# One query tile of two heads at a time in the first block's attention, with the half-array matmuls issued side by side

## The chip, the cores and the metric

The kernel runs on one core of a Trainium2 chip. The metric is the time of one execution in microseconds (us); the median of 3 runs of the kernel before is 2317.44 us (2315.01 to 2317.58). TensorE (PE) multiplies, VectorE (DVE) and ScalarE (ACT) do the elementwise work, GpSimd (POOL) little here, and SyncE (SP) issues most of the DMAs.

## The reference, cut to what matters

Two transformer blocks run one after the other on 256 tokens of width 1024 beside 256 context tokens. The change concerns the first block, which has two layers. Each layer's attention has 8 query heads of 64 numbers and 2 key heads, each shared by 4 query heads. A token sees the context keys and the keys within 128 positions; a learned "sink" joins the sum of each softmax.

```
def sink_softmax(s, sink_b):
    m = jnp.maximum(jnp.max(s, axis=-1, keepdims=True), sink_b)
    e = jnp.exp(s - m)
    return e / (jnp.sum(e, axis=-1, keepdims=True) + jnp.exp(sink_b - m))

s_loc = jnp.where(valid, jnp.einsum('bqkgd,bnkd->bkgqn', qi, ks), -jnp.inf)
s_ctx = jnp.einsum('bqkgd,bnkd->bkgqn', qi, kc)
p = sink_softmax(jnp.concatenate([s_ctx, s_loc], axis=-1), sink_b)
o = einsum('bkgqn,bnkd->bqkgd', p[..., :nc], vc) + einsum('bkgqn,bnkd->bqkgd', p[..., nc:], vs)
```

In the first layer the context tokens are queries as well, over the 256 context keys alone (`context_attention`). In the second layer only the 256 tokens are.

## The kernel before

Activations lie with features on the 128 partitions and tokens along the free dimension. A projection takes each weight as a rounded part and a rest (`wh`, `wl`) and each activation likewise (`xh`, `xl`), and does three matmuls per tile of 128 features (`mm3`, L193 to L195). The parts of a weight chunk are made by ACT (L183) and DVE (L184) from a raw tile that SP's DMA queue has loaded.

The attention is a generator, `attend` (L713), which is advanced by one step each time a projection has finished 128 output columns (`hook`, L731). A step issues `scores` of one call and then `values` of the call before it, so that each softmax has a whole step to finish. A call stands for one pair of heads `t`, one head `hh` of the pair (`t + 4*hh`; head 0 of a pair uses key head 0, head 1 key head 1) and one segment `si`: the 256 tokens (si 0, 512 keys) or the 256 context tokens (si 1, 256 keys, first layer alone). Both 128-row query tiles `i` of the segment are in the call.

`scores` does two matmuls per query tile: one with all 128 rows (L684: the query's rounded part in the head's own 64 rows and its rest in the other 64, against the key's rounded part in both), and one with the head's 64 rows alone (L685: the query's rounded part against the key's rest, `klo`). Results lie in tiles `sc`, of which there are two, each a whole PSUM bank; a call of 256 keys puts both of its query tiles into one. DVE adds the band mask (L688) and takes the maximum (L653); ACT takes the exponential (L657). The rows are then scaled, one tile by ACT (L664) and one by DVE (L666).

`values` transposes the probabilities on PE (L701, 4 or 2 per query tile), has ACT copy one tile and DVE the other from PSUM to `PT` (L702), and then multiplies (L707): weights are 64 columns of `vtok`, so half of the array's columns work, the stream is `PT` with 256 columns, and the sum runs over 4 or 2 blocks of keys. Head 0 writes partitions 0 to 63 of `pso`, head 1 partitions 64 to 127.

A scheduler orders the instructions of each engine by program order and priorities; other matmuls, of the projections and of the modulation vectors (L312, with 32-column weights), are put between the parts of a step. Those L312 matmuls are written so that four consecutive ones use four different strips of 32 array columns.

Of the kernel before, what the change touches and what calls it, by code (L numbers as in the profile page):

```python
# [7 lines left out]
F32 = mybir.dt.float32  # L8
F32R = mybir.dt.float32r
AF = mybir.ActivationFunctionType  # L10
ALU = mybir.AluOpType
AX = mybir.AxisListType
PSUM = bass.MemoryType.PSUM

P = 128
D = 1024
KT = 8
N = 256
T = 512
XS = slice(0, 256)  # L20
CS = slice(256, 512)
# [23 lines left out]
SA = 1  # L45
# [77 lines left out]
class Kern:  # L123
# [67 lines left out]
    def mm3(self, ps, wh, wl, xh, xl, start, stop):  # L191
        mm = self.nc.tensor.matmul
        mm(ps, wh, xh, start=start, stop=False)  # L193
        mm(ps, wh, xl, start=False, stop=False)  # L194
        mm(ps, wl, xh, start=False, stop=stop)  # L195

    def acc(self):
        return self.pacc.tile([P, T], F32, name="acc", tag="acc")
# [380 lines left out]
    def fb_layer(self, l, stats, bga, bgb, AB):  # L579
        nc, I, tc = self.nc, self.I, self.tc  # L580
# [12 lines left out]
        nseg = len(qsegs)  # L593
        fb = self.fb
# [7 lines left out]
        for g in range(4):  # L602
            o = (g % 2) * 64
            nc.scalar.dma_start(wf[o:o + 64, g // 2, o:o + 64], I["w_fourier"][l, g])
        sk = fb.tile([P, 2, 8], F32, name="sk")
        nc.scalar.dma_start(sk[:, 0], I["sink"][l:l + 1, :].to_broadcast([P, 8]))
        nc.vector.tensor_scalar(sk[:, 1], sk[:, 0], -1.0, None, ALU.mult)

        rtmp = lambda: fb.tile([P, 2, T], F32, name="E", tag="E", bufs=EB).rearrange("p a (b n) -> p (a b) n", n=N)
        rows = [slice(0, 64), slice(64, 128)]  # L610
        fr = lambda nm, w_=T: fb.tile([P, w_], F32R, name=nm, tag=nm)
        kh, klo = [fr("kh0"), fr("kh1")], fr("klo")
        vtok = fb.tile([P, 4, P], F32, name="vtok")
        c01 = [self.col(0), self.col(1)]

        def ev_kv(i, ps):
# [7 lines left out]
            else:  # L624
                vT = fb.tile([P, T], F32, name="vT", tag="E", bufs=EB)
                nc.scalar.copy(vT, ps)
# [9 lines left out]
        qs = [[fr(f"qs{t}{j}", TW) for j in range(2)] for t in range(4)]  # L636
# [9 lines left out]
        def q_proj(c, korder=False, hook=None):  # L646
            self.proj(headchunk(0, c), c01, xn, qsegs, lambda i, ps: ev_q(i, ps, c), korder=korder, hook=hook, alloc=None if upd else self.facc)

        def softmax(pss, width, E, h):

            sm = fb.tile([P, 4, 2], F32, name="sft", tag="sft", bufs=3)
            for i, ps in enumerate(pss):
                nc.vector.reduce_max(sm[:, 0, i:i + 1], ps, axis=AX.X)  # L653
            nc.vector.tensor_scalar(sm[:, 1], sm[:, 0], -0.125, sk[:, 1, h:h + 1], ALU.mult, ALU.min)
            nc.vector.tensor_scalar(sm[:, 3], sm[:, 1], sk[:, 0, h:h + 1], None, ALU.add)
            for i, ps in enumerate(pss):
                nc.scalar.activation(E[:, i, 0:width], ps, AF.Exp, bias=sm[:, 1, i:i + 1], scale=0.125,  # L657
                                     accum_out=sm[:, 2, i:i + 1])
            nc.scalar.activation(sm[:, 3], sm[:, 3], AF.Exp)
            nc.vector.tensor_tensor(sm[:, 2], sm[:, 2], sm[:, 3], ALU.add)  # L660
            nc.vector.reciprocal(sm[:, 2], sm[:, 2])
            for i in range(2):
                if i < SA:
                    nc.scalar.activation(E[:, i, 0:width], E[:, i, 0:width], AF.Copy, scale=sm[:, 2, i:i + 1])  # L664
                else:
                    nc.vector.tensor_scalar(E[:, i, 0:width], E[:, i, 0:width], sm[:, 2, i:i + 1], None, ALU.mult)  # L666

        def scores(t, hh, si):
            seg = qsegs[si]
            nk = 4 if si == 0 else 2  # L670
            E = fb.tile([P, 2, T], F32, name="E", tag="E", bufs=EB)
            pss = []
            for i in range(2):
                if si == 0:
                    ps = self.sc()
                elif i == 0:
                    p1 = self.sc()
                    ps = p1[:, 0:256]
                else:
                    ps = p1[:, 256:512]  # L680
                q = qs[t][hh][:, seg.start + i * P:seg.start + (i + 1) * P]
                ks = slice(0, T) if si == 0 else CS
                r = rows[hh]
                nc.tensor.matmul(ps, q, kh[hh][:, ks], start=True, stop=False)  # L684
                nc.tensor.matmul(ps, q[r], klo[r, ks], start=False, stop=True)  # L685
                if si == 0:
                    b = slice((1 - i) * P, (2 - i) * P)
                    nc.vector.tensor_tensor(ps[:, b], ps[:, b], band[:, i * P:(i + 1) * P], ALU.add)  # L688
                pss.append(ps)
            softmax(pss, nk * P, E, t + 4 * hh)  # L690
            return E

        def values(t, hh, si, E, pso):
            seg = qsegs[si]
            nk = 4 if si == 0 else 2
            wd = nk * P
            PT = fb.tile([P, 4, N], F32, name="PT", tag="PT", bufs=2)
            for i in range(2):
                p2 = self.wk()
                for j in range(nk):  # L700
                    nc.tensor.transpose(p2[:, j * P:(j + 1) * P], E[:, i, j * P:(j + 1) * P], self.ident)  # L701
                (nc.scalar.copy if i == 0 else nc.vector.tensor_copy)(  # L702
                    PT[:, 0:nk, i * P:(i + 1) * P], p2[:, 0:wd].rearrange("p (j n) -> p j n", j=nk))
            r = slice(64 * hh, 64 * hh + 64)
            for j in range(nk):
                jj = j if si == 0 else j + 2
                nc.tensor.matmul(pso[r, seg], vtok[:, jj, 64 * hh:64 * hh + 64], PT[:, j, :],  # L707
                                 start=(j == 0), stop=(j == nk - 1))
            if hh == 1 and si == nseg - 1:
                att[t] = f1(f"qs{t}0", TW)  # L710
                nc.scalar.copy(att[t], pso[:, 0:TW])

        def attend():  # L713
            last = None
            for t in range(4):
                pso = None
                for hh in range(2):
                    for si in range(nseg):
                        E = scores(t, hh, si)
                        if last is not None:  # L720
                            values(*last)
                        if pso is None:
                            pso = self.wk()
                        last = (t, hh, si, E, pso)
                        yield
            values(*last)
            yield

        att_gen = attend()

        def hook():  # L731
# [17 lines left out]
        def fourier():  # L749
            for si, seg in enumerate(qsegs):  # L750
                U = fb.tile([P, 2, 2, 2 * P], F32, name="U", tag="PT", bufs=2)
                for tt in range(2):
# [39 lines left out]
        if l == 0:  # L792
# [4 lines left out]
            pss = [[self.facc() for _ in c01] for _ in first]  # L797
# [41 lines left out]
        h = self.xn  # L839
# [32 lines left out]
        ys = [fb.tile([P, 2, T], F32, name="E", tag="E", bufs=EB) for _ in range(3)]  # L872
        ys.append(fb.tile([P, 4, N], F32, name="PT", tag="PT", bufs=2).rearrange("p (a b) n -> p a (b n)", a=2))
        y = [ys[k // 2][:, k % 2, 0:TW] for k in range(KT)]
# [277 lines left out]
    def even_mixer(self, stats):  # L1152
# [10 lines left out]
        with tc.tile_pool(name="ev", bufs=1, reuse_waits="tile") as ev:  # L1163
# [118 lines left out]
            def mlstm():  # L1282
                for hh in range(4):
# [3 lines left out]
                    for dr in range(2):  # L1287
# [3 lines left out]

                        mk = ev.tile([P, 4, P], F32, name="mk", tag="PT", bufs=2)
                        nc.vector.tensor_tensor(mk, pm.rearrange("p (t n) -> p t n", t=4),
# [92 lines left out]
            def dattn(units):  # L1386
                for h, sis in units:
                    c0, hc = h // 2, h % 2
                    for si in sis:
                        nk = 4 if si == 0 else 2  # L1390
                        wd = nk * P
                        for i in range(2):
# [17 lines left out]
                            for j in range(nk):  # L1410
                                nc.tensor.transpose(p2[:, j * P:(j + 1) * P], E[:, 0, j * P:(j + 1) * P], self.ident)
                            PT = ev.tile([P, 4, P], F32, name="PT", tag="PT", bufs=2)
                            (nc.scalar.copy if i else nc.vector.tensor_copy)(PT[:, 0:nk], p2[:, 0:wd].rearrange("p (j n) -> p j n", j=nk))
# [344 lines left out]
```

## Time and profile before

| what | value |
|---|---|
| median of 3 runs | 2317.44 us |
| profiled execution | 2319.22 us |
| its span, first to last instruction | 2317.4 us |
| PE busy | 2243.0 us (97%) |
| DVE busy | 1546.5 us (67%) |
| ACT busy | 892.0 us (38%) |
| mean granted TensorE clock | 0.987 |
| attention of the first layer | 76 to 261 us |
| attention of the second layer | 400 to 472 us |

A row of the profile's time order gives a start, a duration, engine, line and operation. Matmuls are pipelined: a duration includes the time in which a result drains, and the next matmul starts before it ends. What one matmul costs the engine is therefore read as the distance from its start to the start of the next. A full 32-bit matmul (L707, L312) shows as two records, since it takes two passes; the rounded kinds (L193 to L195, L684, L685) show as one.

### The profile page before, as it was taken

To read this page: it belongs to the slowest core of one execution; us is meant where nothing else is said; L and a number is where in the kernel's file an instruction comes from. 1 tells how busy PE (TensorE), PEld (TensorE's weight loads), DVE (VectorE), ACT (ScalarE), POOL (GpSimd) and SP (SyncE) were. 2 spreads that over 40 slices of the span, in tenths; PEclk is the share of its full clock that TensorE was granted. 3 is DMA by queue.
4 is the path that set the end of the run, shared out by engine and by line. 5 is a ranking of instruction groups with operands and counts; after the bars stand their busy time and mean duration, and the time that the engine had idled before them with its cause. 6 is when DMAs were issued, how large, how long until landed. Compare 5 with 4: busy or idle time off the path is not lost.

```text
span 2317.4 us, 33109 instructions
## 1 busy us (share of the span) xinstructions
PE 2243.0 (97%) x13111; PEld 1893.1 (82%) x13111; DVE 1546.5 (67%) x3348; ACT 892.0 (38%) x1645; POOL 50.3 (2%) x113
## 2 busy tenths in 40 slices
PE   6999989999999999999999999999999999999998
PEld 4766687698888899876898888898888897778998
DVE  4644557675999967666769933367859564646555
ACT  3433545564222235444442132342222245534444
POOL 1000000000000000000000000000000000000000
PEclk8999999999999999999999999999999999999999
DMA  8334436654565623211335523244648332124553
GB/s 296 110 118 155 122 93 219 180 155 145 197 195 189 216 86 109 74 37 55 122 103 189 192 91 106 89 155 137 200 144 273 119 119 91 55 74 135 194 182 128
DMA packets 299178, 327.25 MB, mean 141 GB/s; under 512 B 9260, under 2 KB 290916, under 8 KB 295952
## 3 DMA queue, kind: packets, MB, share of 16 engines
q1 hardware_dynamic: 295968, 321.16, 43.0%
q8 instruction: 103, 1.69, 0.3%
q10 hardware_dynamic: 1952, 2.29, 0.3%
q0 software_dynamic: 1104, 1.70, 0.2%
q14 instruction: 51, 0.42, 0.1%
HBM read 324.07 MB, written 1.05 MB: 140 GB/s over the span
## 4 chain that ended last, share of the span: by engine, by line
PE 50%; issue 40%; DVE 5%; ACT 2%; DMA 2%; POOL 1%; SPq 0%; POOLq 0%; DVEq 0%; ACTq 0%
PE acc L193 9%; PE acc L194 9%; PE acc L195 8%; PE sc L193 3%; PE sc L194 3%; PE sc L195 3%; PE wk L707 2%; DVE wl L184 2%; PE acc L312 1%; PE acc L1088 1%; PE acc L1090 1%; PE acc L1089 1%; DMA wr<-in_w_in_dram 1%; PE wk L701 1%; PE sc L1399 1%
## 5 line engine op out<-in xcount | busy, mean ns | idle before, releaser
L193 PE MATMUL acc<-xh,wh 128*128 128x256 f32 (+1 forms) x1792 | 613.1, 343 | 14.5 <-DVE qs L644 4.9
L195 PE MATMUL acc<-xh,wl 128*128 128x256 f32 (+1 forms) x1792 | 606.5, 339 | 5.5 <-DVE wl L184 5.4
L194 PE MATMUL acc<-xl,wh 128*128 128x256 f32 (+1 forms) x1792 | 608.6, 340 | 1.7 <-DVE xl L416 1.6
L183 ACT CAST wh<-wr 128x1024 fp32r<-128x1024 f32 (+1 forms) x394 | 385.9, 1024 | 559.0 <-PE acc L194 261.6
L184 DVE TENSOR_TENSOR wl<-wr,wh 128x1024 fp32r<-128x1024 f32 (+1 forms) x394 | 455.3, 1192 | 159.1 <-ACT wh L183 157.1
L193 PEld LDWEIGHTS acc<-xh,wh 128*128 128x128 f32 x1792 | 343.4, 192 | 73.0 <-issue 24.5
L194 PEld LDWEIGHTS acc<-xl,wh 128*128 128x128 f32 x1792 | 344.7, 192 | 42.6 <-issue 7.1
L195 PEld LDWEIGHTS acc<-xh,wl 128*128 128x128 f32 x1792 | 343.9, 192 | 42.8 <-DVE wl L184 6.4
L283 DVE SCALAR_TENSOR_TENSOR macc<-mraw,vec,macc 128x256 f32<-128x256 f32 x728 | 310.6, 483 | 2.4
L193 PE MATMUL sc<-xh,wh 128*128 128x256 f32 (+1 forms) x816 | 272.0, 334 | 6.8 <-ACT xh L415 4.0
L194 PE MATMUL sc<-xl,wh 128*128 128x256 f32 (+1 forms) x816 | 270.5, 332 | 0.4 <-DVE xl L416 0.4
L195 PE MATMUL sc<-xh,wl 128*128 128x256 f32 (+1 forms) x816 | 270.9, 332 | 0.0
L193 PEld LDWEIGHTS sc<-xh,wh 128*128 128x128 f32 x816 | 156.1, 191 | 22.7 <-ACT xh L415 4.7
L194 PEld LDWEIGHTS sc<-xl,wh 128*128 128x128 f32 x816 | 155.5, 191 | 14.9 <-DVE xl L416 0.9
L195 PEld LDWEIGHTS sc<-xh,wl 128*128 128x128 f32 x816 | 155.7, 191 | 14.2 <-DVE wl L178 0.2
L193 PE MATMUL acc<-hh,wh 128*128 128x256 f32 (+1 forms) x494 | 164.1, 332 | 0.0
L194 PE MATMUL acc<-hl,wh 128*128 128x256 f32 (+1 forms) x494 | 163.9, 332 | 0.0
L195 PE MATMUL acc<-hh,wl 128*128 128x256 f32 (+1 forms) x494 | 163.9, 332 | 0.0
L1020 ACT CAST hh<-hf 128x512 fp32r<-128x512 f32 (+1 forms) x92 | 50.1, 547 | 205.4 <-DVE hf L1015 205.4
L193 PE MATMUL sc<-hh,wh 128*128 128x256 f32 (+1 forms) x354 | 117.6, 332 | 0.0
L195 PE MATMUL sc<-hh,wl 128*128 128x256 f32 (+1 forms) x354 | 117.4, 332 | 0.0
L194 PE MATMUL sc<-hl,wh 128*128 128x256 f32 (+1 forms) x354 | 117.2, 331 | 0.0
(397 smaller groups left out, 2960.4 us busy)
## 6 DMA issues: line engine op xcount, KB each, us to landing
wr<-in_ffn_w_in_dram SPq DMA_DIRECT2D x92, 1024.0 KB, 5.1
mraw<-in_ada_w_dram SPq DMA_DIRECT2D x60, 1024.0 KB, 5.1
wr<-in_ffn_w_out_dram SPq DMA_DIRECT2D x32, 1024.0 KB, 5.1
wr<-in_ffn_w_out_dram SPq DMA_DIRECT2D x22, 768.0 KB, 4.3
xr<-in_w_mod_dram SPq DMA_DIRECT2D x14, 1024.0 KB, 5.5
wr<-in_even_w_in_dram SPq DMA_DIRECT2D x12, 1024.0 KB, 5.4
wr<-in_odd_w_in_dram SPq DMA_DIRECT2D x12, 1024.0 KB, 5.3
wr<-in_w_mod_dram SPq DMA_DIRECT2D x10, 1024.0 KB, 7.1
```

Of the source, the lines that this page charges most:

```text
L183: nc.scalar.copy(hi[:, a:b], raw[:, a:b])
L184: nc.vector.tensor_tensor(lo[:, a:b], raw[:, a:b], hi[:, a:b].bitcast(F32), ALU.subtract)
L193: mm(ps, wh, xh, start=start, stop=False)
L194: mm(ps, wh, xl, start=False, stop=False)
L195: mm(ps, wl, xh, start=False, stop=stop)
L283: nc.vector.scalar_tensor_tensor(a, raw[:, k], cs[:, v * 8 + k:v * 8 + k + 1], a, ALU.mult, ALU.add)
L312: ins = nc.tensor.matmul(ps[32 * j:32 * j + 32, 0:cw], vec[:, k], raw[:, k - k0, j * cw:(j + 1) * cw], start=(k == 0), stop=(k == KT - 1))
L701: nc.tensor.transpose(p2[:, j * P:(j + 1) * P], E[:, i, j * P:(j + 1) * P], self.ident)
L707: nc.tensor.matmul(pso[r, seg], vtok[:, jj, 64 * hh:64 * hh + 64], PT[:, j, :], start=(j == 0), stop=(j == nk - 1))
L1020: nc.scalar.copy(h[0][:, sl], hf)
L1088: mm(o, xn[k][0][:, s], hi[:, k, :], start=(k == 0), stop=False)
L1089: mm(o, xn[k][0][:, s], lo[:, k, :], start=False, stop=False)
```

## The change

A call now stands for one query tile `i` of both heads of a pair. The half-array matmuls of the two heads are issued next to each other: in `scores`, the 64-row matmul of head 0 (rows 0 to 63) and of head 1 (rows 64 to 127), into two different `sc` tiles; in `values`, for each block of keys, head 1 (columns 64 to 127) and head 0 (columns 0 to 63). The new `row` issues a list of matmuls in a given order. The number of calls stays: 16 of 512 keys and 8 of 256. The value matmuls stream 128 columns each and are twice as many. A call of 256 keys now takes both `sc` tiles, and the two small softmax operations with the sink take two columns of `sk`, one for each head. The step order is tokens, tokens, context, context for each pair; before it was tokens, context, tokens, context.

```diff
+    def row(self, mms, after=None):
+        for args, kw in mms:
+            if after is None:
+                after = self.nc.tensor.matmul(*args, **kw)
+            else:
+                with self.tc.issue_after(after.ins):
+                    after = self.nc.tensor.matmul(*args, **kw)
+        return after
...
-            nc.vector.tensor_scalar(sm[:, 1], sm[:, 0], -0.125, sk[:, 1, h:h + 1], ALU.mult, ALU.min)
-            nc.vector.tensor_scalar(sm[:, 3], sm[:, 1], sk[:, 0, h:h + 1], None, ALU.add)
+            nc.vector.scalar_tensor_tensor(sm[:, 1], sm[:, 0], -0.125, sk[:, 1, t:t + 5:4], ALU.mult, ALU.min)
+            nc.vector.tensor_tensor(sm[:, 3], sm[:, 1], sk[:, 0, t:t + 5:4], ALU.add)
...
-                nc.tensor.matmul(ps, q, kh[hh][:, ks], start=True, stop=False)
-                nc.tensor.matmul(ps, q[r], klo[r, ks], start=False, stop=True)
+            pss = [self.sc()[:, 0:nk * P] for _ in range(2)]
+            q = [qs[t][hh][:, seg.start + i * P:seg.start + (i + 1) * P] for hh in range(2)]
+            full = [((pss[hh], q[hh], kh[hh][:, ks]), dict(start=True, stop=False)) for hh in (1, 0)]
+            half = [((pss[hh], q[hh][rows[hh]], klo[rows[hh], ks]), dict(start=False, stop=True)) for hh in (0, 1)]
+            self.row(full + half)
...
-                nc.tensor.matmul(pso[r, seg], vtok[:, jj, 64 * hh:64 * hh + 64], PT[:, j, :],
-                                 start=(j == 0), stop=(j == nk - 1))
+            self.row([((pso[r, o], vtok[:, j if si == 0 else j + 2, r], PT[:, hh, j]), dict(start=(j == 0), stop=(j == nk - 1)))
+                      for j in range(nk) for hh, r in ((1, rows[1]), (0, rows[0]))])
...
-                for hh in range(2):
-                    for si in range(nseg):
-                        E = scores(t, hh, si)
+                for si in range(nseg):
+                    for i in range(2):
+                        E = scores(t, si, i)
```

On PE, a step of the first layer that issues scores of 256 keys and values of 512 stood like this before. `kh_350` with `qs_356` is head 0, L312 is the modulation.

```order
L684 MATMUL sc<-kh_350,qs_356 128x256
L685 MATMUL sc<-klo,qs_356 128x256
L684 MATMUL sc<-kh_350,qs_356 128x256
L685 MATMUL sc<-klo,qs_356 128x256
L701 MATMUL wk<-ident,E 128x128 x8
L312 MATMUL acc<-wr,cst_130 32x512 x2
L707 MATMUL wk<-PT,vtok 64x256 x4
L312 MATMUL acc<-wr,cst_130 32x512 x2
```

The same place now (lines are moved: L201 and L204 are in `row`, L704 is the transpose, L322 the modulation). `kh_350` and `qs_356` are head 0, `kh_351` and `qs_357` head 1.

```order
L201 MATMUL sc<-kh_351,qs_357 128x256
L204 MATMUL sc<-kh_350,qs_356 128x256
L204 MATMUL sc<-klo,qs_356 128x256
L204 MATMUL sc<-klo,qs_357 128x256
L704 MATMUL wk<-ident,E 128x128 x8
L322 MATMUL acc<-xr,cst_130 32x512 x2
L201 MATMUL wk<-PT,vtok 64x128
L204 MATMUL wk<-PT,vtok 64x128 x7
L322 MATMUL acc<-xr,cst_130 32x512 x2
```

The two full matmuls come first and the two halves follow each other; the value matmuls stand in one run of 8 that alternates between the heads, with the same fill-in before and behind.

A step of the first layer that issues scores of 512 keys and values of 512 keys is new, since before these two kinds took turns there. It stands so on PE:

```order
L201 MATMUL sc<-kh_351,qs_357 128x512
L204 MATMUL sc<-kh_350,qs_356 128x512
L204 MATMUL sc<-klo,qs_356 128x512
L204 MATMUL sc<-klo,qs_357 128x512
L704 MATMUL wk<-ident,E 128x128 x8
L322 MATMUL acc<-wr,cst_130 32x512 x4
L193 MATMUL acc<-xh_109,wh 128x512
L194 MATMUL acc<-xl_110,wh 128x512
L195 MATMUL acc<-xh_109,wl 128x512
L201 MATMUL wk<-PT,vtok 64x128
L204 MATMUL wk<-PT,vtok 64x128 x7
```

Four modulation matmuls and three of a projection stand between transposes and values.

On DVE, rows of a first-layer step before, where the copy is of a call of 256 keys (L654 and L655 prepare the exponential):

```order
L688 TENSOR_TENSOR sc<-sc,band 128x128 x2
L653 TENSOR_REDUCE sft<-sc 128x1 x2
L702 COPY PT<-wk 128x2x128
L654 TENSOR_SCALAR sft<-sft,sk 128x2
L655 TENSOR_SCALAR sft<-sft,sk 128x2
```

And of the step of the new kind, where it is of 512 keys:

```order
L692 TENSOR_TENSOR sc<-sc,band 128x128 x2
L663 TENSOR_REDUCE sft<-sc 128x1 x2
L705 COPY PT<-wk 128x512
L664 SCALAR_TENSOR_TENSOR sft<-sft,sk 128x2
L665 TENSOR_TENSOR sft<-sft,sk 128x2
```

Both mask additions and both maxima stand ahead of the copy of the transposes in both; the copy is twice as long now.

## Rows read from the trace of the kernel before

**Rows 1.** Stages: their length, then busy us of each engine, granted clock, DMA

```profile
74.00:257.00 183.00, 180.06 (x873) 116.67 (x871) 82.36 (x207) 66.55 (x155) 0.31 (x1) 1.00 0.38 128
257.00:265.00 8.00, 3.36 (x21) 1.92 (x18) 2.92 (x9) 4.35 (x8) 0.00 (x0) 1.00 0.47 134
400.00:476.00 76.00, 76.00 (x503) 54.45 (x502) 48.04 (x121) 41.72 (x89) 0.00 (x0) 1.00 0.53 153
476.00:2317.00 1841.00, 1809.61 (x10580) 1571.27 (x10578) 1278.87 (x2684) 682.93 (x1187) 35.94 (x67) 0.99 0.42 136
```

**Rows 2.** Order of time on PE, second layer: start us, us, line, operation, sizes

```profile
433.72 0.39 PE L684 MATMUL sc<-kh,qs 128*128 128x512 f32 x1
434.04 0.49 PE L685 MATMUL sc<-klo,qs 64*128 64x512 f32 x1
...
434.90 0.50 PE L685 MATMUL sc<-klo,qs 64*128 64x512 f32 x1
435.33 1.09 PE L701 MATMUL wk<-ident,E 128*128 128x128 f32 x8
...
438.25 1.94 PE L707 MATMUL wk<-PT,vtok 128*64 128x256 f32 x8
440.12 0.39 PE L193 MATMUL acc<-xh,wh 128*128 128x256 f32 x1
```

**Rows 3.** Order of time on PE, first layer

```profile
240.60 0.39 PE L194 MATMUL acc<-xl,wh 128*128 128x512 f32 x1
240.83 0.39 PE L195 MATMUL acc<-xh,wl 128*128 128x512 f32 x1
...
244.23 1.08 PE L707 MATMUL wk<-PT,vtok 128*64 128x256 f32 x4
245.24 0.62 PE L312 MATMUL acc<-xr,cst 128*32 128x256 f32 x4
...
251.37 0.28 PE L684 MATMUL sc<-kh,qs 128*128 128x256 f32 x1
251.57 0.38 PE L685 MATMUL sc<-klo,qs 64*128 64x256 f32 x1
...
252.51 0.33 PE L701 MATMUL wk<-ident,E 128*128 128x128 f32 x1
```

**Rows 4.** The value matmul's line: weight loads, matmuls, count, duration ns min/median/max

```profile
L707 PEld LDWEIGHTS wk<-PT,vtok x160: 132/137/137, 93.7 to 471.7; 128*64 128x64 f32 x160
L707 PE MATMUL wk<-PT,vtok x160: 379/379/430, 93.7 to 471.9; 128*64 128x256 f32 x160
```

**Rows 5.** Order of time on PE, second block: 64-row matmuls issued side by side

```profile
1045.91 1.13 PE L1399 MATMUL sc<-dqk 64*128 64x512 f32 x4
1046.97 0.39 PE L1088 MATMUL acc<-wh,xh 128*128 128x256 f32 x1
```

**Rows 6.** Order of time on PE, second block: 64-column matmuls issued side by side

```profile
2039.17 0.65 PE L1644 MATMUL sc<-S,qe 128*64 128x256 f32 x4
2039.75 0.38 PE L193 MATMUL acc<-xh,wh 128*128 128x256 f32 x1
```

**Rows 7.** Order of time on PE, second block: full 32-bit matmuls of 128 columns

```profile
969.92 1.05 PE L1326 MATMUL sc<-mq 64*128 64x128 f32 x8
970.90 0.71 PE L1342 MATMUL wk<-V,E 128*128 128x130 f32 x4
```

**Rows 8.** Order of time on DVE, second layer

```profile
435.43 0.30 DVE L688 TENSOR_TENSOR sc<-sc,band 128x128 f32<-128x128 f32 x1 [0.24 <-PE sc L685]
435.64 1.28 DVE L653 TENSOR_REDUCE sft<-sc 128x1 f32<-128x512 f32 x2
436.84 0.68 DVE L702 COPY PT<-wk 128x512 f32<-128x512 f32 x1
...
446.22 2.36 DVE L184 TENSOR_TENSOR wl<-wr,wh 128x1024 fp32r<-128x1024 f32 x2 [0.44 <-ACT wh L183]
...
451.38 0.42 DVE L744 COPY gf<-acc 128x256 f32<-128x256 f32 x1 [0.17 <-PE acc L195]
```

More of the change, by code (lines that the diff above doesn't have):

```diff
@@ L647, in q_proj, with softmax @@
             self.proj(headchunk(0, c), c01, xn, qsegs, lambda i, ps: ev_q(i, ps, c), korder=korder, hook=hook, alloc=None if upd else self.facc)
-        def softmax(pss, width, E, h):
+        def softmax(pss, width, E, t):
             sm = fb.tile([P, 4, 2], F32, name="sft", tag="sft", bufs=3)
-            for i, ps in enumerate(pss):
-                nc.vector.reduce_max(sm[:, 0, i:i + 1], ps, axis=AX.X)
-            nc.vector.tensor_scalar(sm[:, 1], sm[:, 0], -0.125, sk[:, 1, h:h + 1], ALU.mult, ALU.min)
-            nc.vector.tensor_scalar(sm[:, 3], sm[:, 1], sk[:, 0, h:h + 1], None, ALU.add)
-            for i, ps in enumerate(pss):
-                nc.scalar.activation(E[:, i, 0:width], ps, AF.Exp, bias=sm[:, 1, i:i + 1], scale=0.125,
-                                     accum_out=sm[:, 2, i:i + 1])
+            for hh, ps in enumerate(pss):
+                nc.vector.reduce_max(sm[:, 0, hh:hh + 1], ps, axis=AX.X)
+            nc.vector.scalar_tensor_tensor(sm[:, 1], sm[:, 0], -0.125, sk[:, 1, t:t + 5:4], ALU.mult, ALU.min)
+            nc.vector.tensor_tensor(sm[:, 3], sm[:, 1], sk[:, 0, t:t + 5:4], ALU.add)
+            for hh, ps in enumerate(pss):
+                nc.scalar.activation(E[:, hh, 0:width], ps, AF.Exp, bias=sm[:, 1, hh:hh + 1], scale=0.125,
+                                     accum_out=sm[:, 2, hh:hh + 1])
             nc.scalar.activation(sm[:, 3], sm[:, 3], AF.Exp)
@@ L661, in softmax @@
             nc.vector.reciprocal(sm[:, 2], sm[:, 2])
-            for i in range(2):
-                if i < SA:
-                    nc.scalar.activation(E[:, i, 0:width], E[:, i, 0:width], AF.Copy, scale=sm[:, 2, i:i + 1])
-                else:
-                    nc.vector.tensor_scalar(E[:, i, 0:width], E[:, i, 0:width], sm[:, 2, i:i + 1], None, ALU.mult)
-        def scores(t, hh, si):
+            for hh in range(2):
+                if hh < SA:
+                    nc.scalar.activation(E[:, hh, 0:width], E[:, hh, 0:width], AF.Copy, scale=sm[:, 2, hh:hh + 1])
+                else:
+                    nc.vector.tensor_scalar(E[:, hh, 0:width], E[:, hh, 0:width], sm[:, 2, hh:hh + 1], None, ALU.mult)
@@ L669, in scores @@
+        def scores(t, si, i):
             seg = qsegs[si]
             nk = 4 if si == 0 else 2
+            ks = slice(0, T) if si == 0 else CS
             E = fb.tile([P, 2, T], F32, name="E", tag="E", bufs=EB)
[L672 to L683, printed above, removed]
-                nc.tensor.matmul(ps, q, kh[hh][:, ks], start=True, stop=False)
-                nc.tensor.matmul(ps, q[r], klo[r, ks], start=False, stop=True)
-                if si == 0:
-                    b = slice((1 - i) * P, (2 - i) * P)
+            pss = [self.sc()[:, 0:nk * P] for _ in range(2)]
[3 more added lines that the diff above has]
+            self.row(full + half)
+            if si == 0:
+                b = slice((1 - i) * P, (2 - i) * P)
+                for ps in pss:
@@ L688, in scores, with values @@
                     nc.vector.tensor_tensor(ps[:, b], ps[:, b], band[:, i * P:(i + 1) * P], ALU.add)
-                pss.append(ps)
-            softmax(pss, nk * P, E, t + 4 * hh)
+            softmax(pss, nk * P, E, t)
             return E
-        def values(t, hh, si, E, pso):
+        def values(t, si, i, E, pso):
             seg = qsegs[si]
@@ L696, in values @@
             wd = nk * P
-            PT = fb.tile([P, 4, N], F32, name="PT", tag="PT", bufs=2)
-            for i in range(2):
+            PT = fb.tile([P, 2, 4, P], F32, name="PT", tag="PT", bufs=2)
+            for hh in range(2):
                 p2 = self.wk()
                 for j in range(nk):
[L701 to L706, printed above, removed]
-                nc.tensor.matmul(pso[r, seg], vtok[:, jj, 64 * hh:64 * hh + 64], PT[:, j, :],
-                                 start=(j == 0), stop=(j == nk - 1))
-            if hh == 1 and si == nseg - 1:
+                    nc.tensor.transpose(p2[:, j * P:(j + 1) * P], E[:, hh, j * P:(j + 1) * P], self.ident)
+                (nc.scalar.copy if hh == 0 else nc.vector.tensor_copy)(
+                    PT[:, hh, 0:nk], p2[:, 0:wd].rearrange("p (j n) -> p j n", j=nk))
+            o = slice(seg.start + i * P, seg.start + (i + 1) * P)
+            self.row([((pso[r, o], vtok[:, j if si == 0 else j + 2, r], PT[:, hh, j]), dict(start=(j == 0), stop=(j == nk - 1)))
+                      for j in range(nk) for hh, r in ((1, rows[1]), (0, rows[0]))])
+            if i == 1 and si == nseg - 1:
                 att[t] = f1(f"qs{t}0", TW)
@@ L723, in attend @@
                             pso = self.wk()
-                        last = (t, hh, si, E, pso)
+                        last = (t, si, i, E, pso)
                         yield
```

## The prediction

> **What bounds the kernel now.** I read the stages first, then the order of time on PE in both layers' attention, then places elsewhere in the kernel where half-array matmuls already stand side by side, and last DVE's order. In the stages the reader is to see that PE has next to nothing idle where the attention runs: 180.1 of 183 us in the first layer, 76.0 of 76 in the second, and 1809.6 of 1841 in all that follows [rows 1]. Between them lie 8 us with PE busy for 3.4: it waits there for the weights of the last gate chunk, whose buffer the last modulation matmuls in the attention set free. DVE is busy for 48 and ACT for 42 of the 76 us. So what is taken from PE's own queue in the attention comes off the time, as long as nothing else moves up into its place.
>
> In the order of time the price of a matmul is the distance to the next start. Two full matmuls of 512 columns follow each other by 0.23 us [rows 3]. A scores call of 512 keys (full, half, full, half) takes from 433.72 to 435.33, 1.61 us, where four times 0.23 would be 0.92: each change between the whole array and half of its rows costs about 0.1 at its end and as much again for weights that are loaded in the open. A call of 256 keys takes 1.14 [rows 3]. A values call of eight records takes 1.87 [rows 2], one of four 1.01 [rows 3]; that is 0.215 for a record of 256 columns and 0.15 for going into the half-array and out. The line has 160 records [rows 4], 16 calls of eight and 8 of four.
>
> **The change part by part.** *Scores.* Before: full to half 0.32, then 0.43 to whatever is next [rows 2]; of 256 columns 0.20, and (1.14 - 0.20) / 3 = 0.31 [rows 3]. Now full, full, half and half together: 0.23 + 0.32 + 0 + 0.43 = 0.98 for 512 keys, 0.63 less; 0.12 (half of 0.23, an estimate) + 0.20 + 0 + 0.31 = 0.63 for 256 keys, 0.51 less. 16 x 0.63 + 8 x 0.51 = 14.2 us less. The 0 for the second half rests on a pair of 64-row matmuls in the second block: four records of 512 columns, two for each, take 1.06 [rows 5]. One of 128 columns takes about 0.12 [rows 7], so one of 512 about 0.49: four in a row would be 1.96, and 1.06 is the time of two. That pair is of the full 32-bit kind; the rounded kind, which streams about twice as fast (0.23 for 512 columns), stands nowhere in a pair. If it doesn't overlap, the second half costs what a full one does: 16 x 0.23 + 8 x 0.12 = 4.6 us back. I take 0, for the nearer row.
>
> *Values.* A pair of 64-column matmuls, two records each, takes 0.58 from 2039.17 to 2039.75 [rows 6]; four such records that are not in pairs take 1.01 [rows 3]. So columns pair too. New is the length of 128. Half of 0.215 is 0.108, and eight records of 128 columns take 0.98 with the way out [rows 7], at most 0.12 each; I take 0.11. A call then has 8 x 0.11 + 0.15 = 1.03 instead of 1.87, and 4 x 0.11 + 0.15 = 0.59 instead of 1.01: 16 x 0.84 + 8 x 0.42 = 16.8 us less. The bounds: with 0.108, 17.2; with no overlap 16 x 0.11 + 0.15 = 1.91 and 8 x 0.11 + 0.15 = 1.03, which is 0.8 us more than before in all.
>
> *The rest.* Transposes, copies, exponentials and their counts stay. The two small operations with the sink change their form at the same two columns; 24 calls of each on an engine with 28 of 76 us idle [rows 1]: 0. Context calls now take both score tiles; the calls of 512 keys did so before, and in the second layer every call is one, with PE idle nowhere: 0.
>
> *What is late next.* The values wait for DVE's copy of the transposes, behind masks and maxima of the newer call. Before: last half issued at 434.90, second mask addition 435.43, maxima 435.64, copy 436.84 to 437.52 [rows 2, 8]; values began at 438.25, 0.73 later. Now both scores are there at once, the last half issued 0.55 into the call. From there 0.53 to the first mask addition, 0.21 for it, then 435.43 to 437.52 as before, 2.09: the copy ends 3.38 into the call (before 3.80). With the same fill-in the values would start 4.53 - 0.63 = 3.90 into it, still 0.5 behind. This chain is hidden by the matmuls put between transposes and values. Where these are few, PE waits for some tenths: the first layer's context calls have only two modulation matmuls there, as they had before, and about four calls of the second layer have a little less than they need. I put 1 us on it in all (bounds 0 and 10, which is 0.4 in each of the 24 calls).
>
> Weights: the last part of a chunk was ready at 446.22 + 2.36 = 448.58, and the tile ahead of its first use was evicted at 451.38 [rows 8]. Of these 2.8 us the gain of one scores and two values calls between its load and its use takes 0.63 + 2 x 0.84 = 2.3. The cover holds; were it gone, some tenths for each chunk. DMA is busy for 0.53 there [rows 1].
>
> In sum 14.2 + 16.8 - 1.0 = 30.0 us. From the profiled execution, 2319.2 (span 2317.4 and 1.8 around it), this gives 2289.2; the median of the runs is 1.8 lower, so 2287.5, rounded to 2288.
>
> **A rule against it.** All of a values call's matmuls use all 128 rows, and in the trace a record of 256 columns takes 0.215 although its weights are loaded for 0.137 [rows 4]: the load is hidden by the matmul ahead of it. The Trainium skill, "TensorE: Matmul & The Clock Gate", Part 3, "The mechanism", says that weight loads overlap with running matmuls only when the row group differs. By that rule each slot of a pair would pay its load, which is the third rival below; the row contradicts it for one column half at a time, and no row shows a longer run that alternates between two halves.
>
> **The rivals.**
> 1. *The gain is given back in waits.* PE catches up with masks, maxima and copies, or with the weights, in most calls. For it: DVE's chain has 0.5 us of cover, and the fill-in was set by a scheduler, not by these times. Against: PE waits for none of this now. 10 us back: 2298.
> 2. *The new pairs don't overlap.* For it: rounded 64-row pairs and runs of alternating column halves stand nowhere in the trace. Against: [rows 5, 6]. If only the columns fail, 14.2 - 0.8 - 1 = 12.4 remain: 2305. If the rows fail as well, 7.8: 2310.
> 3. *Weights can't be loaded while the other half runs.* Each slot is 0.11 + 0.137: 8 x 0.247 + 0.15 = 2.13 and 1.14, 0.26 and 0.13 over before; 16 x 0.26 + 8 x 0.13 = 5.2; 14.2 - 5.2 - 1 = 8: 2309. Against: [rows 4, 6].
> 4. *Slower: each change between column halves empties the array,* as going into half-array work does now (0.15). Sixteen records then take 16 x 0.26 = 4.2 instead of 1.87, eight 2.1 instead of 1.01: 16 x 2.3 + 8 x 1.1 = 45 more against 14 less, so 2348. It is decided at 0.042 us a change, where 0.8 + 320 x 0.042 uses up the 14.2. For it: a change of form does cost this. Against: in [rows 6] two changes of half leave no trace.
> 5. *The gain is swallowed behind the attention* by a transfer that sets its own pace: about 2316. Against: the 1841 us behind have 31 us of PE idle in all, and loads there are released by buffers that PE empties.
>
> **How the numbers follow.** The forecast 0.70, its own range 2281 to 2296; rival 1 0.13, rival 2 0.06, rival 3 0.03, rival 4 0.04, rival 5 0.04. A measurement of this kernel can't tell 0.2%, 4.6 us, from no change. Faster: 0.70 + 0.13 + 0.06 + 0.03 = 0.92; same 0.04; slower 0.04. The range reaches from 2280 (no wait, and slots at their lower bound) to 2306, which takes in rival 1 and the columns of rival 2.
>
> **What would show it.** In the changed profile: scores calls near 0.98 and 0.63 us from first start to the next line's start, with the two halves' starts together; values calls near 1.03 and 0.59, their records in pairs 0.11 apart; PE still without idle time in the second layer's attention, which ends some 12 us earlier counted from its beginning; the rest of the kernel as long as it was. Values records evenly 0.055 to 0.06 apart with the call at 1.9 would show rival 2 or 3; 0.26 apart, rival 4; idle time ahead of the value matmuls that a copy ends, rival 1.

## The result and the profile after

The changed kernel takes 2284.3 us (median; 2280.6 to 2285.7), the kernel before 2317.5 in the same session: a ratio of 0.9861, 95% interval 0.9849 to 0.9873, so 32 us less (0.0139 of 2317). The forecast was 2288 with 2280 to 2306. The profiled execution took 2283.4 with a span of 2281.2, 36.2 under the span of before. 1.6 of these lie ahead of the first changed instruction and belong to no edit.

The stages first, as in [rows 1]: start and end, length, then busy us (and instructions) of PE, PE's weight loads, DVE, ACT and POOL, granted clock, DMA share, GB/s. The rows are the first layer's attention, the stretch to the second layer's, that one, and the rest.

```profile
74.00:236.00 162.00, 156.83 (x968) 111.02 (x966) 77.96 (x208) 66.82 (x157) 0.31 (x1) 1.00 0.44 147
236.00:375.00 139.00, 122.68 (x820) 106.43 (x818) 98.73 (x231) 72.54 (x156) 3.56 (x12) 0.93 0.52 161
375.00:436.00 61.00, 60.91 (x532) 47.78 (x533) 43.83 (x116) 37.84 (x82) 0.00 (x0) 1.00 0.58 175
436.00:2281.00 1845.00, 1813.39 (x10610) 1575.09 (x10608) 1280.32 (x2688) 685.37 (x1193) 35.65 (x67) 0.99 0.43 137
```

PE is as full as it was: 157 of 162 us, and 60.9 of 61. The stages are shorter. From the first score matmul to the last value matmul the first layer takes 162.0 us (before 184.2) and the second 60.0 (71.4); the stretch between them 138.9 (140.2), all behind 1845.7 (1845.5). The granted clock is 1.00 in both attention stages, as before, so the clock gives nothing there. In the stretch between them it is 0.93, before 0.94.

Next, a step of the first layer in order of time on PE: start, duration, engine, line, operation, tile, array shape, sizes. It answers to [rows 2, 3].

```profile
122.38 0.39 PE L201 MATMUL sc<-kh,qs 128*128 128x512 f32 x1
122.61 0.40 PE L204 MATMUL sc<-kh,qs 128*128 128x512 f32 x1
122.93 0.50 PE L204 MATMUL sc<-klo,qs 64*128 64x512 f32 x2
123.37 1.09 PE L704 MATMUL wk<-ident,E 128*128 128x128 f32 x8
124.39 1.06 PE L322 MATMUL acc<-wr,cst 128*32 128x512 f32 x8
125.39 0.50 PE L193 MATMUL acc<-xh,wh 128*128 128x512 f32 x1
...
126.28 0.32 PE L201 MATMUL wk<-PT,vtok 128*64 128x128 f32 x1
126.29 0.32 PE L204 MATMUL wk<-PT,vtok 128*64 128x128 f32 x1
126.44 0.27 PE L201 MATMUL wk<-PT,vtok 128*64 128x128 f32 x1
126.45 0.93 PE L204 MATMUL wk<-PT,vtok 128*64 128x128 f32 x13
127.31 1.99 PE L757 MATMUL wk<-four,uf 128*128 128x256 f32 x8
```

The scores call lasts from 122.38 to 123.37, 0.99 us; both 64-row matmuls are in the one row at 122.93, start 4 ns apart, and hold the engine for 0.44, as one did. The values call lasts from 126.28 to 127.31, 1.03, and 7 ns lie between the starts of head 1 and head 0. Its records come in pairs 0.11 apart. The line of the values after, as in [rows 4] (duration min/median/max in ns, first and last start):

```profile
L204 PEld LDWEIGHTS wk<-PT,vtok x272: 132/137/230, 93.2 to 435.4; 128*64 128x64 f32 x136
L204 PE MATMUL wk<-PT,vtok x272: 272/273/421, 93.2 to 435.5; 128*64 128x128 f32 x136
```

The load takes 137 ns as before, and a pair with two such loads comes every 0.11 us: both loads are hidden.

Summed over all calls, first start to the next line's start, scores went from 34.8 to 21.8 us and values from 38.0 to 21.4. That is 29.6 less. Something else shrank too. Here is the modulation's line alone, the same 192 records in the first layer's attention (length, busy us of PE and of its weight loads, clock, DMA). First before:

```profile
74.00:262.00 188.00, 24.10 (x192) 5.80 (x192) 1.00 0.38 129
```

Then after, where the layer's last modulation matmul also lies within these 188 us:

```profile
74.00:262.00 188.00, 18.53 (x192) 4.94 (x192) 0.98 0.45 146
```

That is 5.6 us less busy, in matmuls that no line of the change touches (25.9 to 20.8 counted from start to next start, 22.6 to 17.4 without the waits that follow some of them). The order of time of before shows why. A group of four such matmuls uses four strips of 32 columns that run at once. Before, two matmuls of a group often stand on either side of the values:

```profile
132.18 1.05 PE L312 MATMUL acc<-wr,cst 128*32 128x512 f32 x4
133.16 1.94 PE L707 MATMUL wk<-PT,vtok 128*64 128x256 f32 x8
135.03 1.05 PE L312 MATMUL acc<-wr,cst 128*32 128x512 f32 x4
136.01 1.99 PE L755 MATMUL wk<-four,uf 128*128 128x256 f32 x8
```

Each half group (two matmuls of two records) takes 0.98: 132.18 to 133.16 and 135.03 to 136.01. In the rows of after above, a whole group of eight records and the same 512 columns takes 1.00, from 124.39 to 125.39. A cut group pays the time of a whole one twice. By the order of the instructions 9 groups of this stage were cut before and 2 are now.

Behind this stage it goes the other way. From there to the end of the second layer's attention 2 groups were cut before and 4 are now, one of 512 columns and one of 256 more. The two parts of the one with 512, after:

```profile
373.82 1.05 PE L322 MATMUL acc<-wr,cst 128*32 128x512 f32 x2
...
376.58 1.06 PE L322 MATMUL acc<-wr,cst 128*32 128x512 f32 x6
377.57 0.39 PE L193 MATMUL acc<-xh,wh 128*128 128x256 f32 x1
```

Two records of this group hold PE for 1.05 from 373.82, and the other six take 0.99, 376.58 to 377.57, as long as all eight would. With the group of 256 columns (0.55 more) that takes 1.6 us back.

Last, PE's waits in the first layer's attention up to its last values: who waits for whom, us in total, times, longest. First before:

```profile
PE acc L193 <- DVE qs L644: 2.9, 1, 2.9
PE wk L322 <- ACT mrow L319: 0.5, 1, 0.5
PE wk L701 <- ACT E L664: 0.2, 1, 0.2
```

Then after:

```profile
PE acc L193 <- DVE qs L654: 3.4, 1, 3.4
PE wk L704 <- ACT E L674: 1.5, 1, 1.5
```

Both kernels have 0.2 more, for a copy to `PT`. The sum rises by 1.3 us. What grew most is the wait for the scaled rows at the end of the stage, from 0.2 to 1.5: the last two calls are now both of 256 keys, little stands between them, and the transposes at 234.56 wait. From the first score to the last value matmul of the second layer PE waits for nothing, before and after.

### The profile page after: what moved, and what is told of

Read it like the earlier page. It is cut to its first block, busy times and chain, and to the rows that moved or that the text cites. A ratio compares the mean times of both kernels' runs of the same rounds, so it can differ in the third digit from the quotient of the medians.

```text
span 2281.2 us, 33404 instructions
## 1 busy us (share of the span) xinstructions
PE 2207.0 (97%) x13271; PEld 1882.1 (83%) x13271; DVE 1540.7 (68%) x3348; ACT 891.0 (39%) x1645; POOL 50.0 (2%) x113
## 3 DMA queue, kind: packets, MB, share of 16 engines
HBM read 324.07 MB, written 1.05 MB: 143 GB/s over the span
## 4 chain that ended last, share of the span: by engine, by line
PE 49%; issue 41%; DVE 5%; ACT 2%; DMA 2%; POOL 1%; SPq 0%; POOLq 0%; DVEq 0%; ACTq 0%
PE acc L193 9%; PE acc L194 9%; PE acc L195 9%; PE sc L193 3%; PE sc L194 3%; PE sc L195 3%; DVE wl L184 2%; PE acc L322 1%; PE acc L1090 1%; PE acc L1092 1%; PE acc L1091 1%; PE wk L704 1%; PE sc L1401 1%; ACT wh L183 1%; PE wk L1344 1%
```

## The experiments

Each was timed against the kernel before. Differences between two changed kernels are differences of such ratios times 2317 us; each ratio is uncertain by about 0.0013, so a difference by about 4 us. The sums of calls come from the profiles and are much sharper.

**Values one head after the other.** Changed kernel, with only the order in the list turned:

```diff
-                      for j in range(nk) for hh, r in ((1, rows[1]), (0, rows[0]))])
+                      for hh, r in ((1, rows[1]), (0, rows[0])) for j in range(nk)])
```

> The changed kernel, but each head's value matmuls stand together, so that no two column halves follow each other; scores stay side by side. Theory (the values' gain is the overlap of the halves): a values call takes 16 x 0.11 + 0.15 = 1.9 us and 1.03 us where the changed kernel shows 1.02 and 0.59; 16 x 0.88 + 8 x 0.44 = 17.6 us more than the changed kernel, so about 2302. Rival (the gain comes from the new order of the calls and fill-in, not from the overlap): within 4 us of the changed kernel, 2280 to 2289.

Measured: 2292.8, ratio 0.9902 (0.9890 to 0.9915), 9.5 us over the changed kernel: between the two. In order of time on PE, a call of 16 records and one of 8:

```profile
103.81 0.43 PE L201 MATMUL wk<-PT,vtok 128*64 128x128 f32 x2
104.08 1.31 PE L204 MATMUL wk<-PT,vtok 128*64 128x128 f32 x14
105.32 0.50 PE L195 MATMUL acc<-xh,wl 128*128 128x512 f32 x1
...
111.74 0.32 PE L201 MATMUL wk<-PT,vtok 128*64 128x128 f32 x1
111.75 0.32 PE L204 MATMUL wk<-PT,vtok 128*64 128x128 f32 x1
...
112.33 0.44 PE L332 MATMUL wk<-ident,mrow 128*128 128x128 f32 x2
```

The long call takes 1.51, neither 1.9 nor 1.03; the short one 0.59, as if nothing had been turned. In the short one head 0's first record starts 14 ns after head 1's first, past three records of head 1 that stand ahead of it in the queue. In the long one head 0's first starts 0.49 us after head 1's first, when five of head 1's eight have started; from there to the end of head 1 the two go in pairs. Each half's records are 0.11 apart both while it runs alone and while the two run together, so neither slows the other. A call wholly without overlap was not run; by 0.11 a record it would take the 1.9 that was expected. So two column halves overlap without being neighbours; it fits both calls that a record goes ahead when at most three of the other half wait before it. Neither theory had that. All values calls together take 29.4 against 21.4, which is 8.0 of the 9.5.

**Values in turns of two.** The test of that reading:

```diff
-                      for j in range(nk) for hh, r in ((1, rows[1]), (0, rows[0]))])
+                      for j0 in range(0, nk, 2) for hh, r in ((1, rows[1]), (0, rows[0])) for j in (j0, j0 + 1)])
```

> The changed kernel with its value matmuls in turns of two instead of one: head 1's blocks 0 and 1, head 0's blocks 0 and 1, head 1's 2 and 3, head 0's 2 and 3 (four records of a half, then four of the other). Theory, from the run with the values apart: a half's matmul starts beside the other half's as long as no more than three records of the other wait ahead of it; four in a row leave three behind the one that runs, so all overlaps: values calls 1.02 and 0.59 us, time as the changed kernel, 2283 (0.986 of the kernel before). Rival: only neighbours overlap, and what overlapped in the run with the values apart did so at its one border; here a call of 16 records has three borders of 2 to 3 records each, so about 1.25 to 1.45, 4 to 7 us over the changed kernel: 2287 to 2290, with the 8-record call as before at 0.59.

Measured: 2285.1, 0.9869 (0.9854 to 0.9884), within the uncertainty of the changed kernel. A long call:

```profile
102.14 0.32 PE L201 MATMUL wk<-PT,vtok 128*64 128x128 f32 x1
102.16 0.32 PE L204 MATMUL wk<-PT,vtok 128*64 128x128 f32 x1
...
103.22 0.50 PE L195 MATMUL acc<-xh,wl 128*128 128x512 f32 x1
```

From 102.14 to 103.22, 1.07 us, with the halves 14 ns apart at the start: as a reach of three records foretells, at 0.05 over strict alternation. The rival's 1.25 to 1.45 is out.

**Scores one head after the other.**

```diff
-            self.row(full + half)
+            self.row([full[0], half[1], full[1], half[0]])
```

> The changed kernel, but its four score matmuls stand as before: full, half, full, half; values stay side by side. Theory: a scores call takes 1.60 and 1.14 us again where the changed kernel shows 0.99 and 0.64; 16 x 0.61 + 8 x 0.50 = 13.8 us more than the changed kernel, so about 2298. Rival (new order of the calls and fill-in): 2280 to 2289.

Measured: 2294.7, 0.9909 (0.9896 to 0.9921), 11.1 us over the changed kernel. PE, one call:

```profile
405.34 0.47 PE L201 MATMUL sc<-kh,qs 128*128 128x512 f32 x1
405.74 0.50 PE L204 MATMUL sc<-klo,qs 64*128 64x512 f32 x1
406.17 0.50 PE L204 MATMUL sc<-kh,qs 128*128 128x512 f32 x1
406.60 0.50 PE L204 MATMUL sc<-klo,qs 64*128 64x512 f32 x1
407.03 0.33 PE L704 MATMUL wk<-ident,E 128*128 128x128 f32 x1
```

The shape and price of before are back: 405.34 to 407.03, four matmuls at 0.40 to 0.43 where no two alike follow each other (1.69 here, 1.61 where a projection goes ahead). All scores sum to 35.1 against 21.8, 13.3 more.

**Scores' halves together, but in the same rows.** This splits the scores' gain in two: fewer changes of form, and overlap.

```diff
-            half = [((pss[hh], q[hh][rows[hh]], klo[rows[hh], ks]), dict(start=False, stop=True)) for hh in (0, 1)]
+            half = [((pss[hh], q[hh][rows[0]], klo[rows[0], ks]), dict(start=False, stop=True)) for hh in (0, 1)]
```

> The changed kernel, but both half matmuls of a scores call read rows 0 to 63, so that head 1's second product is another than the reference's. They stand next to each other and can't overlap; the number of changes between whole array and half is that of the changed kernel. Theory (most of the scores' gain is two changes of form less, the overlap is the smaller part): the second half costs what a full matmul of its length does, 0.23 and 0.12; 16 x 0.23 + 8 x 0.12 = 4.6 us more than the changed kernel, about 2289. Rival (the overlap is the whole gain): 13.8 us more, about 2298.

Measured: 2287.8, 0.9888 (0.9875 to 0.9901), 6.3 over the changed kernel. PE:

```profile
408.64 0.39 PE L201 MATMUL sc<-kh,qs 128*128 128x512 f32 x1
408.88 0.40 PE L204 MATMUL sc<-kh,qs 128*128 128x512 f32 x1
409.20 0.73 PE L204 MATMUL sc<-klo,qs 64*128 64x512 f32 x2
409.87 0.33 PE L704 MATMUL wk<-ident,E 128*128 128x128 f32 x1
```

The two halves hold the engine from 409.20 to 409.87, 0.67 instead of 0.44: 0.23 more, the price of a full matmul of 512 columns. All scores sum to 26.3, 4.6 more than in the changed kernel, the same 4.6 that the prediction had put on this case. So of the scores' 13.0 us, 8.4 come from two changes of form fewer in each call and 4.6 from the overlap.

**Both apart.** Both turned orders in one kernel.

> The changed kernel with both kinds of matmuls apart: what is left against the kernel before is the new order of the calls and of the fill-in. Theory: the two parts add up, 17.6 + 13.8 = 31.4 us more than the changed kernel, 2316, and 1 to 5 us under the kernel before, because fewer groups of four modulation matmuls are cut in two. Rival (the order of the calls costs or gains nothing): equal to the kernel before, 2317, with the parts adding up to 33.

Measured: 2301.9, 0.9945 (0.9933 to 0.9957): 12.7 under the kernel before, where 1 to 5 were expected. The two parts do add up: it is 19.5 over the changed kernel, and the runs above are 9.5 and 11.1 over it. Scores and values sum to 64.0 against 72.7 (8.7 less, since values still overlap partly), and the modulation in the first layer is 6.3 less than before, start to start, 1.1 of it a shorter wait. So something of the gain is no side-by-side work. The next three look for it.

**The kernel before in the changed order of steps.** Nothing but two loops exchanged, so that tokens, tokens, context, context follow each other:

```diff
-                for hh in range(2):
-                    for si in range(nseg):
+                for si in range(nseg):
+                    for hh in range(2):
```

> The kernel before with the order of its steps alone changed: both heads' token calls, then both context calls (tokens, tokens, context, context), as in the changed kernel; the calls themselves are as before. In the order of its instructions the four-strip groups of modulation matmuls in the first layer's attention are now cut about as rarely as in the changed kernel. Theory (the unforeseen 5 us of the changed kernel come from these cuts, and the cuts from the order of the steps): modulation matmuls of that stage 20.8 instead of 25.9 us, scores and values calls as before, time 4 to 6 us under the kernel before: 2310 to 2312 (0.998). Rival (the groups stay whole because the shorter rows of the attention leave the scheduler another place, or their price isn't the cuts): 2315, no change, modulation matmuls at 25 us.

Measured: 2309.8, 0.9978 (0.9969 to 0.9987), 5.1 us under the kernel before. The modulation row of before again, here:

```profile
74.00:262.00 188.00, 19.15 (x192) 5.05 (x192) 1.00 0.39 132
```

19.15 instead of 24.10 (20.7 instead of 25.9 from start to start), with scores and values at 34.75 and 38.0 as before. So the order of the steps alone takes as much off the first layer's modulation as the changed kernel does (5.2 and 5.1 from start to start, 4.6 and 5.1 without waits), through where the scheduler cuts the groups of four: 3 are cut here, against 9 and 2. The rival is out. Not all of it shows in the stage: projections and waits take about 1 us back, and the first layer's attention is 3.7 shorter in the profile (184.2 to 180.5, at a clock of 1.00 in both). How much of the 5.1 is the modulation is therefore known to an us or two only.

**Whole groups in the kernel before.** The other three strips of a group get priority, and are issued right behind its first (`...` stands for the two lines on `pin`, which stay):

```diff
-                    for j in range(4):
-                        ins = nc.tensor.matmul(ps[32 * j:32 * j + 32, 0:cw], vec[:, k], raw[:, k - k0, j * cw:(j + 1) * cw],
-                                               start=(k == 0), stop=(k == KT - 1))
...
+                    strip = lambda j: nc.tensor.matmul(ps[32 * j:32 * j + 32, 0:cw], vec[:, k],
+                                                       raw[:, k - k0, j * cw:(j + 1) * cw],
+                                                       start=(k == 0), stop=(k == KT - 1))
+                    ins = strip(0)
...
+                    for j in range(1, 4):
+                        with self.tc.high_priority(offset=QP), self.tc.issue_after(ins.ins):
+                            ins = strip(j)
```

> The kernel before, with the four modulation matmuls of one block of weights (four strips of 32 array columns) never separated by other matmuls; the attention is as before. In the first layer's attention of the kernel before, four groups of 512 columns stand as 2 and 2, and five of 256 columns are cut as well. Theory (a cut group takes its passes twice: 2 x 0.43 us for 512 columns, 2 x 0.215 for 256, and 0.1 or so for going in and out): 4 x 0.95 + 5 x 0.5 = 6.3 us less than the kernel before, about 2311. Rival (the strips aren't worth it, the rest of the gain is something else): within 1.5 us of the kernel before.

Measured: 2303.2, 0.9945 (0.9931 to 0.9958), 12.7 less, where 6.3 were expected.

```profile
74.00:262.00 188.00, 16.88 (x192) 4.70 (x192) 0.99 0.39 134
```

7.2 us of modulation's busy time go in the first layer, 1.0 in the stretch behind it and 0.4 in the second layer; without waits it is 8.0 in all. That stretch gets 5.2 shorter in this profile: the 1.0, 1.7 less waiting, and some 2.5 in which matmuls that nobody touched run faster. It isn't the whole groups that shorten it, for the kernel with the step order alone has a stretch of 135.9, 4.2 shorter, and its groups there are cut as before. The stretch before, and there:

```profile
260.00:400.00 140.00, 122.27 (x810) 106.95 (x809) 98.16 (x231) 71.67 (x153) 3.57 (x12) 0.94 0.53 161
257.00:393.00 136.00, 119.92 (x811) 104.59 (x810) 97.94 (x230) 71.33 (x153) 3.56 (x12) 0.95 0.53 165
```

The clock has a part in it. In these profiles the granted clock is either 1.00 or 0.50 (2.4 or 1.2 GHz). At the lower level stand 17 us of the stretch before, 14 in the kernel with the step order alone, in this one and in the next, and 20 in the changed kernel. 3.4 us less at half speed are worth at most 1.7. Why PE also waits 1.7 less there isn't settled, and neither is the part of the 12.7 that isn't modulation.

**Whole groups in the changed kernel.**

> The changed kernel, with the same groups of four kept whole. It has one cut group of 512 columns and one of 256 left in the first layer, and three or four in the second. Theory: 0.95 + 4 x 0.5 = 3 us less than the changed kernel if nothing waits in their place, about 2281; the difference between this and the kernel before with whole strips is the gain of the side-by-side matmuls alone, about 30 us. Rival: within 1 us of the changed kernel, because PE then waits for the copies that the cut groups covered.

Measured: 2275.4, 0.9826 (0.9812 to 0.9839), 40 us under the kernel before and 8.1 under the changed one, where 3 were expected; it beats both kernels.

```profile
74.00:262.00 188.00, 16.88 (x192) 4.70 (x192) 0.98 0.45 146
```

In the first layer the modulation comes from 18.53 to the same 16.88. Behind it, up to the end of the second layer's attention, it comes from 15.5 to 12.5, so 4.6 of the 8.1 are modulation without its waits; the stretch at the lower clock is part of the rest. With whole groups on both sides, side by side work alone is 0.9945 to 0.9826, 27.6 us; with the same step order on both sides, 0.9978 to 0.9861, 27.1 us.

## Why the prediction was right, and where it was not

*Scores.* Foreseen 0.98 and 0.63 a call, measured 0.99 and 0.64; 14.2 foreseen, 13.0 measured. Of the 1.2 that lack, 1.0 is in the second layer: two of its calls have modulation matmuls between the two full ones and take 0.34 or 0.43 and then 0.86, and three take 1.06 to 1.08. The 0 for the second half was right: the rounded kind pairs like the 32-bit pair of [rows 5], and the run with the same rows shows the 4.6 that it costs if it doesn't.

*Values.* Foreseen 1.03 and 0.59, measured 1.02 and 0.59; 16.8 and 16.6. Slots of 0.11 for a pair and 0.15 for the way in and out, read from [rows 3, 6, 7], held.

*Waits.* 1 us was put on them, and 1.3 more came, almost all of it at the last call of the first layer. The place was half foreseen (context calls with little between transposes and values), the step order not weighed: two context calls at the end have less between them than a token and a context call.

*The step that failed* is "the same fill-in". Fill-in, the projection and modulation matmuls that stand between the parts of a step, was counted for its cover, not for its own price. That half a group costs as much as a whole one stood in the trace of before. So two terms were left out: 5.1 us gained in the first layer, which come from the order of the steps and not from the halves side by side, and 1.6 lost behind it, where more groups are cut.

*The sum.* 13.0 + 16.6 - 1.3 + 5.1 - 1.6 = 31.8, against 32 by the ratio, which is uncertain by 3. What was foreseen measured 28.3, near the 27.1 and 27.6 that the runs give for the side-by-side work alone. The forecast of 30.0 lies nearer to 32 than its terms earned: it had 1.4 too much on scores and values and 0.3 too little on waits, and 3.5 of unforeseen gain stood against them. That part is luck.

*The rivals.* Waits: 1.3 of the 10 us. No overlap: refuted by starts 4 and 7 ns apart in calls of 0.99 and 1.02 and, for the rows, by the run in the same rows. Weight loads that stay in the open: a call would be 2.13, it is 1.02. The Trainium skill, "TensorE: Matmul & The Clock Gate", Part 3, "The mechanism", lets loads overlap only across row groups; all of a values call uses the same 128 rows, and its loads of 0.137 are hidden in slots of 0.11 for two. The measurement decides. A price for changing halves: a call of eight matmuls takes 1.02 with seven changes, 1.07 with three and 1.51 with one; changing costs nothing that shows, staying does. (The prediction priced it at 320 changes, one for each record; a matmul has two records, and within the calls there are 136.) Swallowed behind the attention: no, 1845.7 us there against 1845.5.

*Left open:* why the stretch between the two attentions gets 4 to 5 us shorter with whole groups or with the step order alone, beyond the part of the clock, and 1.3 us shorter in the changed kernel, which stands longer at the lower clock there.

## What to carry to other kernels

Two matmuls in different halves of the array, in rows or in columns, cost here about what one does if they come close behind each other. For the scores the two changes between whole and half array that went away in each call were worth more than the overlap itself (8.4 and 4.6 of 13.0 us). Before a change to the order of steps is priced, look at what a scheduler will cut: a group of four strips split into two and two pays its time twice, and that is read in the order of instructions before anything runs. Price the fill-in too, not only what is edited.

## What was not expected of the hardware

Matmuls in different column halves don't have to be neighbours. With four records of one half and then four of the other both start within 14 ns; with eight and eight the second half starts 0.49 us late, when three of the first still wait. Weight loads of 137 ns for both halves hide in slots of 0.11 us a pair. A pair of rounded 64-row matmuls of 512 columns takes 0.44 with the way out, in one half 0.67.
